# Other token blocks for the output projection and the FFN of a streaming encoder layer, and seven products for two more rows of the second FFN product

## The chip, the cores and the metric

The kernel runs on one core of a Trainium2 chip, in one launch. The metric is the device time of that execution in microseconds (us). Before the change its median is 2979.64 us over 3 runs (2978.55 to 2980.76).

## The reference

One inference step of one encoder layer, for a prompt of 2048 tokens and a sample of 64 tokens (one prompt, one sample, model width 1024), all in float32. The part that the change touches is the second half of the layer: the gated merge of the two branches, the output projection, and the SwiGLU FFN of inner width 2816 (22 rows of 128).

```
h = rms_norm(x, norm1_g) * (1 + sc1) + sh1
glu_a, glu_b, q, k, v, g_conv, g_attn = split(h @ w_in)
conv_out = conv_module(glu_a * sigmoid(glu_b))        # depthwise, 31 taps, LayerNorm, swish, @ w_conv_out
attn_out = band_attend(q, k, v) @ w_attn_out          # chunks of 64, own chunk and 8 before it

merged = sigmoid(g_conv) * conv_out + sigmoid(g_attn) * attn_out
x = x + gt1 * (merged @ w_o)                          # 1024 x 1024

h2 = rms_norm(x, norm2_g) * (1 + sc2) + sh2
gate, up = split(h2 @ w_ffn_in)                       # 1024 x 5632
x = x + gt2 * ((silu(gate) * up) @ w_ffn_out)         # 2816 x 1024
```

The prompt and the sample use the same weights, but each its own modulation (`sh`, `sc`, `gt`), and the sample has cached keys, values and convolution inputs. The outputs are the new x of both, and the states of convolution and attention.

## The kernel before

**Numbers.** Every float32 matrix is split into two fp32r parts, `hi` (ScalarE copies it) and `lo` (the difference, by VectorE or GpSimd). A product of two split matrices is three matmuls (`mm3`: hi·hi, hi·lo, lo·hi). The 64 sample tokens have a form of their own for the projections of token rows: hi and lo stand side by side as 128 columns, two matmuls (`mm2`) do all four products, and `fold` adds the two halves.

**Two parts.** The first part (up to about 1199 us) makes the modulation, the input projection, convolution, attention and gates, and leaves the branches' inputs and the gates in memory. The second part is a loop over `CBLOCKS`, three blocks of tokens in which the sample's tokens are 0 to 63 and the prompt's 64 to 2111:

```
CBLOCKS = [(0, 576), (576, 1344), (1344, 2112)]
```

The first block has 576 tokens, the sample and four tiles of 128; the other two have 768, six tiles. Each block goes through these stages.

- *Merge and output projection*, in two chunks of tiles. `load_mixed` and `gate_columns` load the inputs (`cin`, `tg`), `merge` multiplies them by the branch weights (`ca`) and joins the gates, and `wo` does the output projection into `pw`.
- *Columns.* For each tile a generator, `residual`, adds x, normalises the row, transposes it (TensorE), applies the modulation, and splits the result into operands for the FFN. The tokens of a block are cut in two halves (`half` columns: 288 in the first block, 384 in the others). From the two halves and the two halves of the model width come four quarters, and from them the seven operands `b11, b21, t2, t3, t1, t4, b22`.
- *Hand-over.* While the last columns are made, TensorE has ten products, `first` and `second`, of 12 matmuls each, for the first `EARLY` = 5 rows f (they need only `b11` and `b21`; their results are kept as `early`). Then the loop begins, which needs all seven operands.
- *Loop* over the 22 rows f, in pairs. `up` makes gate and up of row f by seven products instead of eight (Strassen's scheme in Winograd's form): 84 matmuls of `half` columns (`ps`), with sums of weights s1 to s4. VectorE and ScalarE combine the groups (`plus`, `silu`) and split the result, `hidden`, into `hid`. Between the products of a pair stand those of the pair before into the second FFN matrix (`pd`, 512 wide), whose results VectorE adds to `acc`. They are done in one of two ways. `down` and `add_down` do one product for each tile, column half and row. `down_pair`, where `seven(s, f)` says so, does a pair of rows and two halves of the tokens by seven products; `rest` makes the four sums S1 to S4 of the hidden columns (`sums`) for it, and GpSimd the sums t1 to t4 of the weights. Before, `seven` holds for f = 4 to 19 of the second and third block; its products are three tiles deep.
- *End of a block.* `add_down` or `add_last` adds the last rows, the modulation `gt2` and x, and sends the rows out; `scale` multiplies `acc` on GpSimd ahead of that.

**Weights.** `Weights` loads raw slabs (`wst`, `wup`, `wfo`), splits them (`whi`, `wlo`) and keeps up to five split slabs ahead of use. In the first block the sums s1 to s4 of the first FFN matrix are made on GpSimd (`ws`), used, and stored in memory (`sum_d`); the later blocks read them back. In the first block `W.hold` keeps the splits of these sums until the columns are done. The low half of a slab goes to GpSimd by default, and to VectorE in these cases, of which the last one matters here:

```
late = key[0] in ("up", "fo") and self.stream.load["pool"] - self.stream.load["pe"] > POOL_BEHIND   # 3000 ns
e, name = (self.dve, "dve") if on_dve or late else (self.gps, "pool")
```

**Order of the work.** Every engine runs its instructions in the order in which the program issues them. That order comes from a planner: `Stream` keeps a planned time for each engine (`load`), from a cost for each instruction; `after` and `when` shift it by dependences; generators wait in a `Lane` until TensorE's planned time has reached their due time. `weight_order` writes out the order of the slabs by hand. DMAs are issued on SP's queue.

**Buffers.** Eight banks of PSUM: four of tag `gp`, and `y0`, `z0`, `y1`, `z1`, in which the groups of `up` alternate. `down_pair` takes `zs` (one of `gp`, and `y1`, `z1`) and `ys` (of `gp`), one bank for each tile of a half, and uses each bank for several products in turn.

Of the kernel before, what the change touches and what calls it, by code (L numbers as in the profile page):

```python
# [35 lines left out]
CBLOCKS = [(0, 576), (576, 1344), (1344, 2112)]  # L36
# [41 lines left out]
def tile_chunks(lo, hi):  # L78

    tiles = token_tiles(lo, hi)  # L80
    t, n = tiles[(len(tiles) + 1) // 2 - 1]
    return [(lo, t + n), (t + n, hi)]
# [181 lines left out]
class Weights:  # L264
# [67 lines left out]
    @staticmethod  # L332
    def rows_of(op):

        return {"b11": (0,), "t1": (0,), "t3": (0, 1)}.get(op, (1,))
# [228 lines left out]
def seven(s, f):  # L564


    return s > 0 and 4 <= f < NF - 2
# [7 lines left out]
DOWN_OPERANDS = (("b11", "b21"), ("t3", "t2"), ("t1", "t4"), ("b22",))  # L575
# [8 lines left out]
def weight_order():  # L584
# [10 lines left out]
    for s in range(len(CBLOCKS)):  # L595
# [4 lines left out]
        for f in range(0, NF, 2):  # L600
            ops = up_operands(f) + up_operands(f + 1)
            for j in range(0, len(ops), 2):
                yield ("up", *ops[j : j + 2])
                if f >= 2 and seven(s, f - 2):
                    yield from (("dn", s, f - 2, *DOWN_OPERANDS[i]) for i in {0: (0,), 2: (1, 2), 4: (3,)}.get(j, ()))
                elif j == 0 and f >= 2 and f - 2 not in last_rows(s):
                    yield from (("fo", f - 2), ("fo", f - 1))
# [4 lines left out]
def streaming_layer(ctx: ExitStack, tc: tile.TileContext, I, O):  # L612
# [505 lines left out]
    def gate_columns(c0, c1, ct):  # L1118
        g = [half_piece(ct % 2, "tg") for _ in range(2)]
        for j in range(2):  # L1120
            nc.sync.dma_start(g[j][:, : c1 - c0], g_d[j, ct, :, c0:c1])
        return g

    def load_mixed(c0, c1, i):

        src = [[quarter("cin", i) for _ in range(2)] for _ in range(2)]
        for j, a in enumerate((c_d, o_d)):
            for l in range(2):
                nc.sync.dma_start(src[l][j][:, :, : c1 - c0].bitcast(F32), a[l, :, :, c0:c1].rearrange("c p t -> p c t"))
# [478 lines left out]
    for b, stage in ORDER:  # L1608
# [21 lines left out]
        elif stage == "g":  # L1630
            for g in gates(b, free):
# [6 lines left out]
                if g == SIDE_G and b == len(PBLOCKS) - 1:  # L1638
# [5 lines left out]
                    cs = tile_chunks(*CBLOCKS[0])[0]  # L1644
                    src = load_mixed(*cs, 0)
                    first_gates = gate_columns(*cs, 0)
# [43 lines left out]
    def merge(c0, c1, src, m, ahead, load):  # L1690
        n = c1 - c0
        cut = 0 if c0 else SMP
        for ct in range(KT):
# [15 lines left out]
            if ct + 2 < KT:  # L1709
                ahead.append(gate_columns(c0, c1, ct + 2))  # L1710
            dve.scalar_tensor_tensor(ps[1], ps[1], 2.0, t, ALU.mult, ALU.add)
            stream.after("act", "dve")
            hi = m[0][:, ct, cut : cut + n]
            act.activation(hi, ps[1], AF.Copy)
            stream.after("dve", "act")
            if cut:
                dve.tensor_tensor(m[0][:, ct, :cut], ps[1][:, :cut], hi[:, :cut].bitcast(F32), ALU.subtract)
            dve.tensor_tensor(m[1][:, ct, cut:n], ps[1][:, cut:], hi[:, cut:].bitcast(F32), ALU.subtract)
# [99 lines left out]

    c0, c1 = tile_chunks(*CBLOCKS[0])
    nxt = [first_gates, gate_columns(*c0, 1)]  # L1820
    srcs = [src]
    W.last_phase(wk, sum_d)
    for s, (lo, hi) in enumerate(CBLOCKS):
        tiles = token_tiles(lo, hi)
        half = (hi - lo) // 2
        gt1, groups, hs = {}, [], None
        chunks = tile_chunks(lo, hi)
        for i, (c0, c1) in enumerate(chunks):
            m = [wk.tile([P, KT, CW // 2], F32R, tag=f"m{j}", name="m") for j in range(2)]
            merge(c0, c1, srcs[i], m, nxt, (lambda: srcs.append(load_mixed(*chunks[1], 1))) if len(srcs) == 1 else None)  # L1830
            if c1 < hi:
                nxt = [gate_columns(c1, hi, ct) for ct in range(2)]
            else:
                turns.drain(groups[0], True)
            grp = [(t, n) for t, n in tiles if c0 <= t < c1]
            pss = [[row_bank(i, j) for j in range(2)] for i in range(len(grp))]
            if not groups:
                for which in {int(t < SMP) for t, _ in tiles}:
# [5 lines left out]
            def free():  # L1844
# [4 lines left out]
                residual(pss[i], t, n, gt1, t - lo, half, hs, free, c1 == hi, i) for i, (t, n) in enumerate(grp)  # L1849
# [7 lines left out]
            def wo(i, k):  # L1857
                (t, n), pp = grp[i], pss[i]
# [3 lines left out]
                c = slice(t - c0, t - c0 + n)  # L1862
                a = m[0][:, k, 0 if c0 else SMP :]
                for j in range(2):
                    f = slice(512 * j, 512 * j + 512)
                    if t < SMP:
                        mm2(pp[j], m[0][:, k, : 2 * SMP], wh[:, 0, f], wl[:, 0, f], k == 0, k == KT - 1)
                    else:
                        mm3(pp[j][:n], a[:, c], m[1][:, k, c], wh[:, 0, f], wl[:, 0, f], k == 0, k == KT - 1)
# [4 lines left out]
            shared = KT - 2 if not s and c1 == hi else 4  # L1874
# [3 lines left out]
            for i, (t, n) in enumerate(grp):  # L1878
                for k in range(shared, KT):
                    wo(i, k)  # L1880
                while gens[i] in xs:
                    turns.push()
                next(gens[i])
                turns.add(gens[i])
# [39 lines left out]

        def hidden(f, i, ps):
            h = hid_of(f)
            c = slice(i * half, (i + 1) * half)
            stream.after("act", "dve")
            if s:
                split(h[:, 0, c], h[:, 1, c], ps)  # L1930
                return
            hi = h[:, 0, SMP:][:, c]
            act.activation(hi, ps, AF.Copy)
            stream.after("dve", "act")
            cut = 0 if i else SMP
            if cut:
                dve.tensor_tensor(h[:, 0, :cut], ps[:, :cut], hi[:, :cut].bitcast(F32), ALU.subtract)
            dve.tensor_tensor(h[:, 1, c][:, cut:], ps[:, cut:], hi[:, cut:].bitcast(F32), ALU.subtract)
# [80 lines left out]
        def rest(f, z, y):  # L2019
# [5 lines left out]
            if "t" not in sums:  # L2025
                sums["t"] = wk.tile([P, 4, 2, CW // 2], F32R, tag="m1", name="sums")
            at = lambda i: [sums["t"][:, i, l, :half] for l in range(2)]
            if f % 2 == 0:
                sums["a21"], sums["s3"] = (
                    wk.tile([P, CW // 2], F32, tag=name, name=name, bufs=1)[:, :half] for name in ("a21", "s3")  # L2030
# [266 lines left out]
```

## Time and profile before

| | |
|---|---|
| median of 3 runs | 2979.64 us (2978.55 to 2980.76) |
| the profiled execution's own time | 2979.5 us |
| its span, first to last instruction | 2977.7 us |
| mean granted clock of TensorE | 0.995 |
| second part | from about 1199 us to the end |
| first block: merge and projection, hand-over, loop | 1199 to 1301, 1301 to 1390, 1390 to about 1717 us |
| hand-over of the second and of the third block | around 1865 and 2495 us |

The profile's first part gives the busy time of each engine over the span. PE is TensorE's matmuls, PEld its weight loads, which run beside the matmuls; DVE is VectorE, ACT ScalarE, POOL GpSimd, SP the engine that issues DMAs. The chain that ended last goes back from the last instruction to what released each step. A window row gives the busy time and count of every engine in a stretch, then TensorE's granted clock (1 is full speed), the DMA engines' busy share and GB/s. A row of waits reads: waiting engine and tile, released by which engine and tile, us in total, how many times, longest. A row of the timeline reads: start, duration, engine, operation, with the idle time ahead of it and its releaser in brackets. Rows by form give count, busy us, mean ns of one, and the idle time ahead of them. All operations are recorded by one helper, so all lines are L102; the tiles' names tell them apart.

### The profile page before, as it was taken

What the parts mean: (1) busy time and instruction counts of PE and PEld (TensorE: products, weight loads), DVE (VectorE), ACT (ScalarE), POOL (GpSimd) and SP (SyncE); (2) the same over time, 40 slices, a digit from 0 to 9 for tenths busy, and PEclk for the clock granted to TensorE, in tenths of its full rate; (3) what the DMA queues carried; (4) which work ended last, traced back from release to release, by engine and by line L of the source; (5) the groups of instructions that cost most, each with busy time, mean ns of one, the idle gap of its engine ahead of it and who ended that gap; (6) DMA issues with size and microseconds to landing.
All of it is one profiled execution on the core that took longest, in us unless ns stands there. A gap on an engine that the chain in (4) does not pass through costs nothing.

```text
span 2977.7 us, 44838 instructions
## 1 busy us (share of the span) xinstructions
PE 2900.2 (97%) x16199; PEld 2593.1 (87%) x16199; DVE 2025.9 (68%) x3637; ACT 1356.8 (46%) x2441; POOL 1127.7 (38%) x727
## 2 busy tenths in 40 slices
PE   7999899999999999989999999999999999999999
PEld 4899777787888888888999999999999999999998
DVE  5797677767856886577777755666666557466666
ACT  2345642662456257464444345534444345344442
POOL 0201310111011102454466443255666741465667
PEclk9999999999999999999999999999999999999999
DMA  8889889878987798885444786333333975333333
GB/s 290 300 286 310 270 279 312 284 251 274 306 283 224 267 263 278 262 288 175 145 145 159 244 263 235 116 95 106 114 113 113 316 239 184 93 95 114 114 103 128
DMA packets 467723, 628.05 MB, mean 211 GB/s; under 512 B 36276, under 2 KB 314664, under 8 KB 467501
## 3 DMA queue, kind: packets, MB, share of 16 engines
q1 hardware_dynamic: 453456, 605.58, 62.8%
q10 hardware_dynamic: 14045, 19.60, 1.9%
q8 instruction: 127, 2.08, 0.3%
q14 instruction: 95, 0.78, 0.1%
HBM read 476.53 MB, written 148.54 MB: 210 GB/s over the span
## 4 chain that ended last, share of the span: by engine, by line
PE 82%; DVE 7%; DMA 4%; ACT 2%; issue 2%; POOL 2%; SPq 0%; ACTq 0%; POOLq 0%; DVEq 0%
PE ps L102 53%; PE pd L102 16%; PE pw L102 6%; DVE y L102 2%; PE sc L102 2%; PE po L102 2%; PE ptp L102 2%; DVE wlo L102 1%; PE pt L102 1%; DMA kk<-k_d 1%; ACT whi L102 1%; PE pa L102 1%; POOL r L102 1%; DVE pw L102 1%; DMA wst<-in_w_in 0%
## 5 line engine op out<-in xcount | busy, mean ns | idle before, releaser
L102 PE MATMUL ps<-t,whi 128*128 128x384 f32 (+1 forms) x2112 | 503.1, 322 | 8.7 <-ACT t L102 4.9
L102 POOL TENSOR_TENSOR wlo<-wst,whi 128x1024 fp32r<-128x1024 f32 (+1 forms) x156 | 356.4, 2294 | 279.0 <-ACT whi L102 262.6
L102 ACT ACTIVATE whi<-wst 128x1024 fp32r<-128x1024 f32 (+1 forms) x263 | 256.8, 979 | 331.2 <-PE ps L102 119.8
L102 PE MATMUL ps<-b,whi 128*128 128x384 f32 (+1 forms) x1584 | 381.7, 326 | 7.0 <-DVE early L102 3.6
L102 PEld LDWEIGHTS ps<-t,whi 128*128 128x128 f32 x2112 | 367.8, 188 | 16.3 <-ACT t L102 5.1
L102 DVE SCALAR_TENSOR_TENSOR y<-u,wd,y 128x512 f32<-128x512 f32 (+1 forms) x480 | 369.0, 773 | 6.3
L102 PE MATMUL ps<-hh,whi 128*128 128x512 f32 (+2 forms) x992 | 361.7, 365 | 0.0
L102 DVE TENSOR_TENSOR acc<-acc,pd 128x512 f32<-128x512 f32 x464 | 311.7, 685 | 62.7 <-PE pd L102 60.2
L102 PE MATMUL ps<-hl,whi 128*128 128x512 f32 (+2 forms) x992 | 345.6, 348 | 0.0
L102 PE MATMUL ps<-hh,wlo 128*128 128x512 f32 (+2 forms) x992 | 345.4, 348 | 0.0
L102 PE MATMUL ps<-t,wlo 128*128 128x384 f32 (+1 forms) x1056 | 339.4, 322 | 0.8 <-POOL wlo L102 0.7
L102 PE MATMUL pd<-whi,hid 128*128 128x512 f32 x972 | 314.8, 390 | 0.0
L102 PEld LDWEIGHTS ps<-b,whi 128*128 128x128 f32 x1584 | 278.7, 189 | 13.1 <-DVE early L102 4.5
L102 POOL TENSOR_TENSOR r<-t,mhalf 128x1 f32<-128x1 f32 (+3 forms) x68 | 83.6, 1232 | 462.1 <-DVE t L102 457.0
L102 PE MATMUL ps<-b,wlo 128*128 128x384 f32 (+1 forms) x792 | 257.3, 325 | 0.0
L102 ACT ACTIVATE pr<-pr,sm 128x640 f32<-128x640 f32 (+3 forms) x272 | 200.1, 747 | 112.1 <-DVE sm L102 109.5
L102 PEld LDWEIGHTS pd<-whi,hid 128*128 128x128 f32 x972 | 182.5, 188 | 37.7 <-ACT hid L102 0.7
L102 PEld LDWEIGHTS ps<-hh,wlo 128*128 128x128 f32 x992 | 186.7, 188 | 21.6
L102 PEld LDWEIGHTS ps<-hh,whi 128*128 128x128 f32 x992 | 187.2, 189 | 18.5 <-issue 1.6
L102 PEld LDWEIGHTS ps<-hl,whi 128*128 128x128 f32 x992 | 187.5, 189 | 15.5 <-issue 1.4
L102 PEld LDWEIGHTS ps<-t,wlo 128*128 128x128 f32 x1056 | 198.2, 188 | 2.2 <-POOL wlo L102 1.3
L102 PE MATMUL pd<-wlo,hid 128*128 128x512 f32 x508 | 198.6, 391 | 0.0
(226 smaller groups left out, 6170.6 us busy)
## 6 DMA issues: line engine op xcount, KB each, us to landing
whi<-w_din_h SPq DMA_DIRECT2D x72, 512.0 KB, 6.5
wlo<-w_din_l SPq DMA_DIRECT2D x72, 512.0 KB, 8.4
wst<-sum_d SPq DMA_DIRECT2D x132, 256.0 KB, 2.7
wfo<-in_w_ffn_out SPq DMA_DIRECT2D x64, 512.0 KB, 3.2
wmod<-in_w_ada SPq DMA_DIRECT2D x46, 512.0 KB, 6.5
sum_d<-ws SPq DMA_DIRECT2D x88, 256.0 KB, 2.8
wst<-in_w_ffn_in SPq DMA_DIRECT2D x84, 256.0 KB, 3.1
wst<-in_w_in SPq DMA_DIRECT2D x40, 512.0 KB, 8.8
```

The source lines that it names most:

```text
L102: self.last = f(*args, **kw)
```

## The change

The second part's blocks become 768, 768 and 576 tokens, and the sample moves from the first block to the last, where it stands third among five tiles, across the middle. `seven` starts at f = 2 and holds in the last two blocks, also in the last one with the sample. There the halves have 288 columns, of which `side` = 32 belong to the sample; the seven products run over the `wide` = 256 inner columns of the prompt (two tiles deep), and the sample's rows get `mm2` products of their own (`sample`), for which the slab with `b22` gets an eighth operand, `b12`. `hidden_sample` splits the sample's 32 columns of each half. In `rest`, the split of S3 moves from the even row to the odd one. `scale`, `add_last` and `add_down` follow: the rows `gt` for the sample are loaded in the last block, and `add_last` does its last rows with `mm2` and a fold.

```diff
-CBLOCKS = [(0, 576), (576, 1344), (1344, 2112)]
+CBLOCKS = [(64, 832), (832, 1600), (1600, 2112)]
+MIXED = 2
...
+def block_tiles(s):
+    tiles = [(t, P, t - CBLOCKS[s][0]) for t in range(*CBLOCKS[s], P)]
+    if s == MIXED:
+        tiles = tiles[:2] + [(0, SMP, 2 * P)] + [(t, n, a + SMP) for t, n, a in tiles[2:]]
+    return tiles
+
+def block_chunks(s):
+    lo, hi = CBLOCKS[s]
+    n = (hi - lo) // 2
+    return [[(0, lo, n)] + [(n, 0, SMP)] * (s == MIXED), [(0, lo + n, n)]]
...
 def seven(s, f):
-    return s > 0 and 4 <= f < NF - 2
+    return s > 0 and 2 <= f < NF - 2
...
+def down_operands(s):
+    return ("b11", "b21"), ("t3", "t2"), ("t1", "t4"), ("b22", "b12") if s == MIXED else ("b22",)
...
-            shared = KT - 2 if not s and c1 == hi else 4
+            shared = KT - 2 if len(grp) < 3 else 4
...
+        side = half - 2 * P if s == MIXED else 0
+        wide = half - side
+        inner = [slice(0, wide), slice(side, half)]
...
         def hidden(f, i, ps):
...
+            split(h[:, 0, rows_at[i]], h[:, 1, rows_at[i]], ps[:, inner[i]])
+            hidden_sample(f, i, ps)
...
         def rest(f, z, y):
...
             if f % 2 == 0:
+                hidden_sample(f, 1, whole)
...
-                split(*at(2), y)
                 act.activation(sums["s3"], y, AF.Copy)
                 return
-            hidden(f, 1, y)
-            t = bank("gp")
+            hidden(f, 1, whole)
+            split(*at(2), sums["s3"])
+            t = bank("gp")[:, :wide]
...
         def down_pair(f):
...
-            n = len(tiles) // 2
+            n = wide // P
...
+            def sample(ps, w, es, j):
+                for e, (h, l) in zip(es, ((t[0][:, i], t[1][:, i]) for t, i in w)):
+                    mm2(ps, hid[0][:, e, 0, both], h, l, e == es[0], e == es[1])
+                stream.after("dve", "pe")
+                dst = acc[n][:, 512 * j : 512 * j + 512]
+                dve.tensor_tensor(dst, dst, ps, ALU.add)
...
             products(ys, a11, w, 0, True, False, 0, 0)
             yield
-            zs += [bank_of(tag, "pd") for tag in ("y1", "z1")]
+            zs += [bank_of(tag, "pd") for tag in ("y1", "z1")[: n - 1]]
             products(zs, a12, w, 1, True, True, 0, 0)
+            if s == MIXED:
+                sample(bank_of("gp", "pd"), ((w, 0), (w, 1)), (0, 1), 0)
...
             products(zs, s3, w, 0, True, False, 1, 1)
             yield
             products(ys, s2, w, 1, False, False, 1, 0)
             W.done()
             w = W.get(("dn", s, f, *ops[2]))
             products(ys, s1, w, 0, False, False, 1, 1)
             products(zs, a22, w, 1, False, True, 1, 0)
             W.done()
             yield
             w = W.get(("dn", s, f, *ops[3]))
             products(ys, s4, w, 0, False, True, 0, 1)
+            if s == MIXED:
+                sample(bank_of("z1", "pd"), ((w, 0), (w, 1)), (1, 0), 1)
```

More of the change, by code (lines that the diff above doesn't have):

```diff
@@ L1688, in token_row, with merge @@
         return wk.tile([P, D], F32, tag="row", name=name, bufs=6)
-    def merge(c0, c1, src, m, ahead, load):
-        n = c1 - c0
-        cut = 0 if c0 else SMP
+    def merge(chunk, src, m, ahead, load):
+        n = width(chunk)
+        cut = n - (SMP if len(chunk) > 1 else 0)
         for ct in range(KT):
```

180 lines of the change are left out of this document (96 added, 84 removed).

## The prediction

> **What bounds the kernel now.** I read the page first (span, engines, chain), then the windows stage by stage, then TensorE's waits in the stretches that the change touches, and last the durations by form.
>
> ```profile
> PE 2900.2 (97%) x16199; PEld 2593.1 (87%) x16199; DVE 2025.9 (68%) x3637; ACT 1356.8 (46%) x2441; POOL 1127.7 (38%) x727
> ...
> PE 82%; DVE 7%; DMA 4%; ACT 2%; issue 2%; POOL 2%; SPq 0%; ACTq 0%; POOLq 0%; DVEq 0%
> ```
>
> TensorE is busy for 97% of the span and holds 82% of the chain that ended last. So only two things can move the time: the number and pitch of matmuls, and the few places where TensorE stands. The windows show where in the second part it stands: the hand-over of its first block (1301 to 1390), that block's loop (1390 to 1690), and, for comparison, the loop of the last block (2520 to 2940).
>
> ```profile
> core 0: us, PE busy (x) PEld busy (x) DVE busy (x) ACT busy (x) POOL busy (x), PEclk, DMA share, GB/s
> 1301.00:1390.00 89.00, 77.61 (x488) 71.70 (x487) 68.76 (x122) 49.67 (x96) 40.37 (x31) 0.96 0.74 255
> 1390.00:1690.00 300.00, 297.47 (x1911) 276.74 (x1910) 217.20 (x343) 124.82 (x255) 172.97 (x113) 1.00 0.48 154
> 2520.00:2940.00 420.00, 419.64 (x2201) 392.71 (x2201) 261.26 (x428) 183.06 (x310) 252.41 (x152) 1.00 0.33 104
> 1318.70:1322.30 3.60, 3.35 (x13) 2.92 (x13) 3.10 (x7) 2.23 (x8) 0.00 (x0) 0.53 1.03 396
> 1329.00:1332.40 3.40, 3.34 (x14) 3.35 (x15) 3.40 (x6) 1.12 (x3) 2.70 (x3) 0.52 0.50 185
> ```
>
> The hand-over leaves TensorE idle for 89.00 − 77.61 = 11.4 us, the first loop for 2.5 us, the last block's loop for 0.4 us. The last two rows are stretches right behind idle time, with a granted clock of 0.53 and 0.52: 3.60 × 0.47 + 3.40 × 0.48 = 3.3 us more. The hand-over thus loses 11.4 + 3.3 = 14.7 us. TensorE's waits there, and then at the hand-over to the third block (2470 to 2520):
>
> ```profile
> PE ps L102 <- ACT t L102: 4.9, 1, 4.9
> PE ps L102 <- DVE early L102: 2.6, 1, 2.6
> PE ps L102 <- DVE u L102: 1.6, 1, 1.6
> PE ps L102 <- DVE v L102: 1.4, 1, 1.4
> PE ps L102 <- ACT early L102: 0.8, 2, 0.5
> ```
>
> ```profile
> PE ps L102 <- DVE early L102: 0.5, 1, 0.5
> PE ps L102 <- POOL wlo L102: 0.3, 1, 0.3
> PE ps L102 <- ACT early L102: 0.2, 1, 0.2
> ```
>
> 11.3 us of named waits in the first block stand against 1.0 us in the third. The first makes its weight sums on GpSimd and is 576 tokens wide; the third reads the sums back and is 768 wide. Half of the difference in width is what the change takes away.
>
> **The terms, against the profiled execution (2979.5 us, 1.8 us more than the page's span of 2977.7; the median of the runs, 2979.64, is 0.14 above).**
>
> *Matmuls.* In the order of instructions the first FFN product, merge and output projection keep their matmuls at the same widths, only in another order of blocks. The second FFN product goes from 616, 720 and 720 matmuls to 792, 711 and 562: 2056 to 2065, +9. The wider first block has six full tiles by eight products; the two more rows by seven products and the narrower last block nearly pay for it. The pitch, from 32 and then 20 matmuls in a row, and from 8 at the third width:
>
> ```profile
> 1499.79 0.39 PE L102 MATMUL pd<-whi,hid 128*128 128x512 f32 x1
> ...
> 1507.05 0.39 PE L102 MATMUL pd<-whi,hid 128*128 128x512 f32 x1
> 1507.27 0.42 PE L102 MATMUL ps<-t,whi 128*128 128x288 f32 x2
> ...
> 1509.90 0.29 PE L102 MATMUL ps<-t,wlo 128*128 128x288 f32 x1
> ```
>
> ```profile
> 2199.96 0.51 PE L102 MATMUL ps<-t,whi 128*128 128x384 f32 x2
> ...
> 2201.35 0.33 PE L102 MATMUL ps<-t,wlo 128*128 128x384 f32 x1
> ```
>
> 7.26 / 32 = 0.227 us, 2.63 / 20 = 0.1315 us, 1.39 / 8 = 0.174 us. So 9 × 0.227 = **+2.0 us**: the arithmetic alone makes the kernel slightly slower, and every gain must come from waits.
>
> *Hand-over of the first block.* While ScalarE and VectorE turn the last tiles into columns and their sums, TensorE has the ten products of `first` and `second` to do, 12 matmuls each. At 384 columns these 120 matmuls last 120 × (0.174 − 0.1315) = 5.1 us longer. The second of the long waits, and what ScalarE waits for ahead of it:
>
> ```profile
> 1316.24 1.15 ACT L102 ACTIVATE whi<-ws 128x512 fp32r<-128x512 f32 x2 [2.32 <-POOL ws L102]
> 1318.72 0.73 PE L102 MATMUL ps<-b,whi 128*128 128x288 f32 x2 [2.63 <-DVE early L102]
> ```
>
> The waits are steps of one chain (columns, then operands `t`, then the first groups of the loop), so 5.1 us more cover takes 5.1 of 11.3 us off; both half-clock stretches follow waits of 2.6 us and more, and I let their 3.3 us go with them: −8.4, taken as **−8.5 us**. One end is −13.7 (the first block becomes like the third, 14.7 − 1.0). The other is 0: the second group now has three tiles instead of two, and in the new order ScalarE has three `whi<-ws`, which wait for GpSimd's sums as above, ahead of the columns of the last two tiles. What is late next in either case is that column work. [...]
>
> *Loop of the first block.* Its 2.5 us of idle are VectorE and ScalarE behind a 288-wide step; at 384 every product lasts a third longer, the loops of that width idle 0.4 us in 420. **−2.5 us**, from 0 to −6 (stalls that the modelled ends cover).
>
> *Hand-over of the last block*, now the 288-wide one: the third block's 1.0 us of waits with 5.1 us less cover, but without sums to make. **+1.5 us**, from −1 (sums already stored, five tiles instead of six) to +7 (all of the 5.1 us as a wait, and 1.7 us of half clock behind it). Its sample rows come as extra DMAs of a few per block on SP; they are issued among the loads of the merge, ahead of need by a chunk, and cost nothing unless they delay `cin`, which is in the +7.
>
> *Loop of the last block.* This is the dear unknown. `split` gives the low half of an `up` or `fo` slab to VectorE where GpSimd's planned load is over 3 us ahead of TensorE. With a 288-wide loop that is nearly always: the order of instructions has 80 `wlo` on VectorE in the last block (79 of 1024 elements) where the block before had 25, and the first block 129, mostly of 512. The durations:
>
> ```profile
> L102 DVE TENSOR_TENSOR wlo<-ws,whi 128x512 fp32r<-128x512 f32 x47 | 44.6, 953 | 3.8 <-ACT whi L102 2.6
> ...
> L102 DVE TENSOR_TENSOR hid<-ps,hid 128x288 fp32r<-128x288 f32 x18 | 8.2, 456 | 7.2 <-ACT hid L102 7.2
> ...
> L102 DVE TENSOR_TENSOR hid<-ps,hid 128x224 fp32r<-128x224 f32 x17 | 6.4, 378 | 0.0
> ```
>
> ```profile
> L102 DVE TENSOR_TENSOR acc<-acc,pd 128x512 f32<-128x512 f32 x178 | 120.3, 686 | 18.1 <-PE pd L102 17.0
> ...
> L102 DVE TENSOR_TENSOR wlo<-wst,whi 128x1024 fp32r<-128x1024 f32 x8 | 11.2, 1395 | 2.9 <-ACT whi L102 2.8
> ```
>
> ```profile
> 2702.37 1.28 DVE L102 TENSOR_TENSOR acc<-acc,pd 128x512 f32<-128x512 f32 x2
> ```
>
> A pair of rows f costs TensorE 168 matmuls of the first product and 50 of the second: 168 × 0.1315 + 50 × 0.227 = 33.4 us. VectorE does in it 16 `acc` × 0.686 = 11.0, 7 `wlo` × 1.395 = 9.8, 14 operations of 288 × 0.456 = 6.4, 11 of 256 (between 0.378 and 0.456, so 0.42) = 4.6, and 4 of 32 columns (taken at 0.2, about half of the 0.378) = 0.8: 32.6 us, 98%. Operations queued behind one another overlap, though: two `acc` take 1.28 us where 2 × 0.686 = 1.37, 0.09 less each. With most of 52 so queued that gives back up to 4.6 us: 28 to 30 us, 85 to 90%, where the last block now has 261.26 / 420 = 62% and the first 217.20 / 300 = 72%. So I expect VectorE to keep up, but late adds to bite in one place: with two tiles, the product by S1 re-uses the banks of the product by S2 after only one group of three matmuls (3 × 0.227 = 0.68 us), while the add that must come between lasts 0.69. A `wlo` ahead of it in VectorE's queue makes TensorE wait 0.3 to 1.0 us, and behind that wait the whole loop is queued. At the low end, 9 pairs × 0.33 = **+3.0 us**; from 0 (the add starts in time) to +18 (rival A). The split of S3 that moves to the odd row is used a whole row later, 84 × 0.1315 = 11 us: nothing. GpSimd's own work falls with the slabs it loses.
>
> [...]
>
> *Tail.*
>
> ```profile
> 2971.96 0.39 PE L102 MATMUL pd<-whi,hid 128*128 128x512 f32 x1
> ...
> 2973.63 0.69 DVE L102 TENSOR_TENSOR acc<-acc,pd 128x512 f32<-128x512 f32 x1
> ```
>
> VectorE now ends 2.0 us behind TensorE's last matmul. The tail's matmuls fall from 72 to 56 (16.3 to 12.7 us), its VectorE operations from 24 to 22 (by 0.6 to 0.69 us each, 13.3 to 15 us), so VectorE falls behind: **+1.0 us**, 0 to +2.5.
>
> **Sum:** 2.0 − 8.5 − 2.5 + 1.5 + 3.0 + 1.0 = −3.5 us: **2976.0 us**.
>
> **Rivals.**
>
> *A, VectorE becomes the bound of the last block (slower).* For it: 98% by durations, and the trace has VectorE idle before work it must wait for (18.1 / 178 = 0.10 us before each `acc`, 7.2 / 18 = 0.40 before each 288-wide `hid`): 32.6 + 16 × 0.10 + 4 × 0.40 = 35.8 us a pair, 2.4 more than TensorE; with a little of the overlap given back, about 2. Nine pairs: +18 in place of +3: **2991 us**. Against it: those idle times shrink as soon as a queue stands. It decides when VectorE's busy share in the pairs exceeds some 95%.
>
> *B, the hand-over vanishes and VectorE keeps up.* 2.0 − 13.7 − 2.5, the other terms at nothing: −14.2, **2965 us**. For it: the third block's 1.0 us of waits at the same width. Against it: the third reads stored sums, the first still makes them.
>
> *C, the loss only moves with the 288 columns to the last block.* −8.5 becomes −7 and +1.5 becomes +7, the rest as forecast: 2.0 − 7 − 2.5 + 7 + 3 + 1 = +3.5, **2983 us**. Against it: the second and third blocks make no sums.
>
> That the change does not do what it says is no rival: the counts in the order of instructions are those of its words.
>
> **How the numbers follow.** 0.2% is 6.0 us, about what a measurement of this kernel tells from no change. The forecast's own case (2969 to 2982) gets 0.42, of which 0.13 lies below 2973.6; B 0.27, A 0.24, C 0.07. Faster: 0.27 + 0.13 = 0.40; same: 0.29 + 0.07 = 0.36; slower: 0.24. Range: 2963 (the middle of B and a little beyond) to 2993 (past the middle of A), which leaves out the far halves of A and B, some 0.2.
>
> **What would show it.** In the profile after: TensorE's waits in the first hand-over at 3 to 7 us and no clock of 0.5 in it; 0.5 us or less idle in that block's loop; about 1.5 to 3 us of waits ahead of the last block's loop; in that loop, waits of `pd` matmuls for VectorE's `acc`, a few tenths each, once a pair, and VectorE busy at 85 to 92%. It is wrong if the first hand-over still waits over 10 us, if `ps` matmuls of the last loop wait for VectorE's plus operations or its `wlo` in every row (A), or if a wait on a DMA appears in the last merge.

## The result, and the profile after

The change makes the kernel slower: 3001.61 us median (2999.62 to 3005.45, 4 runs) against 2979.10 us (2978.04 to 2980.76, 4 runs) before, a ratio of 1.0077 with a 95% interval of 1.0059 to 1.0094. The prediction was 2976.0 us, 2963 to 2993.

The page of the kernel after, engines and chain:

```profile
PE 2906.9 (97%) x16208; PEld 2592.6 (86%) x16208; DVE 2058.2 (69%) x3667; ACT 1372.3 (46%) x2516; POOL 1127.4 (38%) x747
...
PE 77%; DVE 11%; DMA 4%; ACT 3%; issue 3%; POOL 1%; SPq 1%; ACTq 0%; DVEq 0%; POOLq 0%
```

TensorE's busy time grew by 6.7 us, and its share of the chain fell from 82% to 77%, that of VectorE rose from 7% to 11%. The windows by stage: the first hand-over with the start of its loop, that loop, the last block's merge, its hand-over with the start of the loop, its pairs of seven products, and two stretches right behind idle time.

```profile
core 0: us, PE busy (x) PEld busy (x) DVE busy (x) ACT busy (x) POOL busy (x), PEclk, DMA share, GB/s
1331.60:1400.00 68.40, 57.99 (x308) 53.95 (x308) 58.59 (x92) 37.95 (x75) 35.21 (x26) 0.98 0.69 234
1400.00:1818.00 418.00, 417.40 (x2203) 392.54 (x2202) 212.45 (x317) 151.54 (x280) 244.99 (x169) 1.00 0.38 123
2478.00:2590.00 112.00, 107.58 (x634) 96.94 (x633) 64.47 (x131) 51.75 (x83) 56.95 (x28) 0.98 0.90 289
2590.00:2652.00 62.00, 52.34 (x339) 48.90 (x338) 40.58 (x74) 36.13 (x67) 14.25 (x9) 0.94 0.49 167
2690.00:2960.00 270.00, 265.85 (x1678) 242.09 (x1677) 242.00 (x401) 147.40 (x304) 149.98 (x97) 1.00 0.43 134
1362.90:1366.40 3.50, 3.48 (x11) 3.48 (x12) 3.50 (x7) 1.58 (x3) 0.00 (x0) 0.54 0.00 0
2612.40:2615.60 3.20, 3.20 (x13) 3.20 (x14) 3.20 (x6) 0.60 (x1) 0.00 (x0) 0.50 0.00 0
```

TensorE stands idle for 10.4 us in the first hand-over, almost the 11.4 of before, and now for 9.7 us in the last block's, where it waited about 1 us before. The last block's pairs lose 4.2 us of 270, and VectorE is busy there for 242 of 270 us, 90%. TensorE's waits in the first hand-over, and then from 2560 to 2690 us:

```profile
PE ps L115 <- ACT early L115: 2.5, 2, 1.4
PE ps L115 <- ACT t L115: 2.2, 1, 2.2
PE ps L115 <- DVE t L115: 1.9, 1, 1.9
PE ps L115 <- DVE u L115: 1.7, 2, 1.4
PE ps L115 <- DVE early L115: 1.6, 2, 1.3
...
```

```profile
PE ps L115 <- ACT t L115: 8.3, 1, 8.3
PE ps L115 <- DMA wlo<-w_dfi_l: 1.1, 1, 1.1
...
```

**Where the time went.** The first part of the kernel, untouched, took from 1190 to 1199 us in the profiled executions of this study. So I also compare the second part alone, from the first merge matmul (`ps<-cin`) to TensorE's last one: 1772.7 us before (1199.2 to 2972.0), 1796.5 us after (1195.2 to 2991.8), +23.8. By blocks, from one block's first merge matmul to the next one's (for the last block, to the end of TensorE's last matmul): 515.8, 628.5 and 628.9 us before, 656.2, 627.2 and 513.6 us after. With the pitch of 0.227 us for the matmuls of the second product (616, 720, 720 before, 792, 711, 562 after), a wide first block should have taken 628.9 + 72 × 0.227 = 645.2 us and took 11.0 more; a narrow last one 515.8 − 54 × 0.227 = 503.5 us and took 10.1 more; the middle one is 0.7 over its 626.5. With the 9 matmuls (2.0) that is 23.8.

A finer table takes the time from each matmul's start to the next one's, less the pitch of its width (0.2268, 0.1735, 0.1305 us for 512, 384, 288), summed by stage; I call it the loss (matmuls missing from a trace count in it, and 0.001 us on the pitch of 288 is 1.8 us in a loop). "Hand-over" is `first` and `second` with the transposes between them, and the first 40 us of the loop:

| us lost | merge, projection | hand-over | rest of loop | end |
|---|---|---|---|---|
| before, first block (576) | 3.5 | 11.1 + 4.4 | 10.0 | 0.0 |
| before, second block (768) | 1.0 | 1.7 + 0.6 | 4.1 | 0.4 |
| before, third block (768) | 1.3 | 1.7 + 0.7 | 4.1 | 0.4 |
| after, first block (768) | 1.3 | 6.5 + 8.4 | 2.9 | 0.0 |
| after, second block (768) | 1.1 | 1.7 + 0.7 | 4.8 | 0.4 |
| after, last block (576) | 7.7 | 10.8 + 2.1 | 17.5 | 0.9 |

All hand-overs together lose 10.0 us more than before (30.2 and 20.2), the loops 7.0 (25.2 and 18.2), the merges 4.3 (10.1 and 5.8), the ends 0.5; with the matmuls' 2.0 that is the 23.8. Each trace is one execution, so differences of a few us in a stage of the last block tell little: e6 and e11 below, whose edits leave that block alone, run it in 509.5 and 508.3 us instead of 513.6; there its hand-over loses 12.5 and 13.0 us (12.9 in the changed kernel), its loop 16.4 and 13.7, its merge 5.1 and 6.1.

The wide block did not lose less by going first than the narrow one had, and the narrow one lost nearly as much again going last.

### The profile page after: what moved, and what is told of

Read it like the earlier page. It is cut to its first block, busy times and chain, and to the rows that moved or that the text cites. A ratio compares the mean times of both kernels' runs of the same rounds, so it can differ in the third digit from the quotient of the medians.

```text
span 2997.5 us, 44910 instructions
## 1 busy us (share of the span) xinstructions
PE 2906.9 (97%) x16208; PEld 2592.6 (86%) x16208; DVE 2058.2 (69%) x3667; ACT 1372.3 (46%) x2516; POOL 1127.4 (38%) x747
## 4 chain that ended last, share of the span: by engine, by line
PE 77%; DVE 11%; DMA 4%; ACT 3%; issue 3%; POOL 1%; SPq 1%; ACTq 0%; DVEq 0%; POOLq 0%
PE ps L115 50%; PE pd L115 13%; PE pw L115 6%; DVE wlo L115 3%; DVE y L115 2%; PE sc L115 2%; PE po L115 2%; PE ptp L115 2%; DVE acc L115 1%; PE pt L115 1%; DVE ps L115 1%; PE pa L115 1%; ACT whi L115 1%; POOL r L115 1%; DVE pw L115 1%
## 5 line engine op out<-in xcount | busy, mean ns | idle before, releaser
L115 PE MATMUL ps<-t,whi 128*128 128x384 f32 (+1 forms) x2112 | 505.3, 323 | 19.4 <-ACT t L115 10.5
L115 ACT ACTIVATE whi<-wst 128x1024 fp32r<-128x1024 f32 (+1 forms) x272 | 264.7, 979 | 285.8 <-PE ps L115 115.7
L115 PEld LDWEIGHTS ps<-t,whi 128*128 128x128 f32 x2112 | 369.1, 188 | 28.4 <-ACT t L115 11.1
L115 POOL TENSOR_TENSOR wlo<-wst,whi 128x1024 fp32r<-128x1024 f32 (+1 forms) x130 | 276.8, 2139 | 217.1 <-ACT whi L115 180.7
L115 DVE TENSOR_TENSOR acc<-acc,pd 128x512 f32<-128x512 f32 x451 | 298.6, 683 | 65.7 <-PE pd L115 64.5
L115 PE MATMUL pd<-whi,hid 128*128 128x512 f32 x1002 | 322.9, 390 | 0.3 <-DVE acc L115 0.3
L115 PEld LDWEIGHTS ps<-b,whi 128*128 128x128 f32 x1584 | 278.3, 189 | 12.6 <-ACT early L115 3.9
L115 DVE TENSOR_TENSOR wlo<-wst,whi 128x1024 fp32r<-128x1024 f32 (+1 forms) x142 | 201.6, 1421 | 91.5 <-ACT whi L115 90.1
L115 POOL TENSOR_TENSOR wlo<-ws,whi 128x512 fp32r<-128x512 f32 x113 | 145.7, 1307 | 209.3 <-ACT whi L115 208.0
L115 POOL TENSOR_TENSOR wlo<-wfo,whi 128x512 fp32r<-128x512 f32 (+1 forms) x92 | 161.9, 1774 | 135.6 <-ACT whi L115 135.6
```

What stands on the lines that cost most here:

```text
L115: self.last = f(*args, **kw)
```

## The experiments

Each median is that of the experiment's own runs, and each ratio is to the kernel before, run again beside them; "second part" is the length defined above, of the profiled execution (1796.5 us after).

**Two parts of the change.** e1 is the kernel before with the rows alone, e2 the changed kernel with the blocks alone.

```diff
# e1, on the kernel before (S3's split on the odd row for f = 2 only)
-    return s > 0 and 4 <= f < NF - 2
+    return s > 0 and 2 <= f < NF - 2
# e2, on the changed kernel (S3's split on the even row)
-    return s > 0 and 2 <= f < NF - 2
+    return s > 0 and 4 <= f < NF - 2
```

> The kernel before with one part of the change alone: seven products from row 2 in the two blocks that have them, blocks as before. 18 matmuls of 512 fewer (2056 to 2038). Theory 1 (the loss comes from VectorE's queue in a 288-wide last block) and theory 2 (the loss is the 288-wide block's hand-over) both say: 18 x 0.227 = 4.1 us faster than before, about 2975. Rival (the second product's new pair and the S3 split taken from SBUF cost as much as they save): 2979 or more.

Measured: 2974.98 us, ratio 0.9984 (0.9974 to 0.9994), second part 1771.3 us. The rows are a small gain; the median agrees with 18 × 0.227, the second part shows 1.4 of the 4.1 us.

> The changed kernel with seven products from row 4 only and S3 split on the even row from PSUM, as before: the blocks' part of the change alone. 15 matmuls more than the changed kernel (+3.4 us). If the blocks carry the loss (theories 1 and 2): 2999 to 3005, at least 20 us over before. If the pair of rows 2 and 3 carries it: near 2980.

Measured: 3002.91 us, ratio 1.0081 (1.0066 to 1.0096), second part 1800.0 us, 3.5 over the changed kernel for 15 matmuls more. The blocks carry the whole loss.

**VectorE as the bound.** e3 takes 0.75 us a pair off VectorE; e4 moves low halves from VectorE to GpSimd, 33 of the last block's 79 by the trace.

```diff
# e3
             if f % 2 == 0:
...
+                if "t" in sums:
+                    split(*at(2), y)
                 act.activation(sums["s3"], y, AF.Copy)
...
-            split(*at(2), sums["s3"])
+            if f == first_seven + 1:
+                split(*at(2), sums["s3"])
# e4, in split
+            late = late and not (i > self.last_start and i % 2)
```

> The changed kernel with S3 split on the even row straight from PSUM in all pairs but the first of a block. In the changed kernel's last block that split's second half, from two SBUF operands, took 1.17 us on VectorE where the other three of 256 columns took 0.42. Theory 1 (VectorE's queue bounds the last loop): 8 x 0.75 = 6 us of VectorE less, so 2996 to 2999. Theory 2: no change, 3001.

Measured: 3004.01 us, ratio 1.0085 (1.0070 to 1.0100), second part 1799.7 us. No gain, although VectorE's busy time in the last block's pairs fell from 242.0 to 231.9 us.

> The changed kernel, but in the last block every second slab of the first product that would go to VectorE stays on GpSimd (34 low halves of 1024 moved back, 1.65 us each on VectorE, 2.4 on GpSimd). Theory 1: VectorE falls from 89% to about 75% of that loop, its excess of some 13 us mostly goes: 2988 to 2993. Theory 2: the loop's loss is not VectorE's, 3000 or more. Rival within theory 1 (GpSimd becomes the bound): waits of matmuls for wlo of GpSimd, 3001 or more.

Measured: 3002.21 us, ratio 1.0077 (1.0062 to 1.0092), second part 1796.8 us. No gain, although the load moved as meant. The last block's pairs in e4, and TensorE's waits in them:

```profile
2690.00:2960.00 270.00, 263.42 (x1686) 241.97 (x1684) 211.48 (x377) 148.78 (x307) 194.39 (x122) 1.00 0.43 133
```

```profile
PE pd L115 <- DVE acc L115: 2.4, 6, 0.4
PE ps L115 <- DVE acc L115: 2.3, 3, 0.8
PE ps L115 <- ACT u L115: 1.8, 2, 1.5
```

VectorE fell from 90% to 78%, and TensorE still waits for its `acc`. A load that can be lowered by an eighth without effect was not the bound: theory 1 falls.

**Banks used again after one group.** In the trace after, the place looks like this (TensorE, then VectorE at the same time):

```profile
2851.93 0.39 PE L115 MATMUL pd<-wlo,hid 128*128 128x512 f32 x1
2852.49 0.50 PE L115 MATMUL pd<-whi,sums 128*128 128x512 f32 x1 [0.17 <-DVE acc L115]
```

```profile
2848.92 0.69 DVE L115 TENSOR_TENSOR acc<-acc,pd 128x512 f32<-128x512 f32 x1
2849.53 1.94 DVE L115 TENSOR_TENSOR wlo<-wst,whi 128x1024 fp32r<-128x1024 f32 x1
2851.40 0.45 DVE L115 TENSOR_TENSOR ps<-ps,u 128x288 f32<-128x288 f32 x1
2851.76 1.27 DVE L115 TENSOR_TENSOR acc<-acc,pd 128x512 f32<-128x512 f32 x2
```

The second matmul, the first with S1, is the one that waits. Two matmuls of the next product (`hid`) already stand ahead of it, so five matmuls, 1.1 us, lie between the two uses of the bank, not the three that the prediction counted; it is so in all six pairs where TensorE waits for `acc`. A `wlo` of 1.94 us stands ahead of the add for which TensorE waits. e7 does not shorten it; it only lets TensorE do another product first.

```diff
+            products(zs, a22, w, 1, False, True, 1, 0)
             products(ys, s1, w, 0, False, False, 1, 1)
-            products(zs, a22, w, 1, False, True, 1, 0)
```

> The changed kernel, with the product of a22 by t4 ahead of that of S1 by t1 in each pair, so that no bank is used again after one group only. The trace after shows 0.33 + 0.11 us once a pair at that place. If it is the bank: 9 x 0.44 = 4 us faster, 2997.6. If VectorE is late in any case (theory 1), the wait moves to the next group: 3001.

Measured: 2995.77 us, ratio 1.0055 (1.0038 to 1.0073), 5.8 below the changed kernel; second part 1789.4 us, 7.1 less; the loss in the rest of the loop falls from 17.5 to 8.0 us. The pairs in e7, and all that TensorE waits for in them:

```profile
2690.00:2960.00 270.00, 269.09 (x1736) 251.08 (x1735) 242.54 (x412) 150.86 (x309) 155.62 (x102) 1.00 0.45 140
```

```profile
PE ps L115 <- ACT u L115: 0.7, 3, 0.3
```

VectorE is as busy as in the changed kernel (242.54 and 242.00 us of 270), and TensorE hardly waits. So 9.5 us of the loop's loss hung on the distance between two uses of a bank. In the table's terms 5.3 us of the changed kernel's loss stood ahead of matmuls with S1 to S4 (0.4 in e7), and 2.5 us where `ps` goes over from `b` to `t` (0.1 in e7). The 8.0 us that stay are less than the 288-wide loop lost before (10.0).

**The last hand-over.** e5 queues the first products that need `t` behind the last `second`; in the changed kernel a matmul that reads `t` stood ahead of 48 that read none.

```diff
+            with tc.issue_after(pe.last.ins) if not f else nullcontext():
                 if not f:
                     z = bank("z0")
                     step(z, "s3", "t3", True, False)
                 step(y, "s2", "t2", f < EARLY, False)
```

> The changed kernel, with the first two products of row 0 queued on TensorE behind the last `second` product. In the changed kernel's last block one matmul that needs the operand t stands ahead of 48 ready matmuls of `first` and `second` and waits 8.3 us. Theory 3 (the loss at the last hand-over is the order of TensorE's queue): the 48 matmuls x 0.1315 = 6.3 us go into that wait and the half clock behind it goes too: 2993 to 2995. Rival (the columns are late and the order is indifferent): 3001.

Measured: 3002.34 us, ratio 1.0073 (1.0058 to 1.0088), second part 1799.5 us. No gain, and the trace tells why: now the sixth product, which needs no `t`, waits as long.

```profile
2601.89 0.29 PE L115 MATMUL ps<-b,wlo 128*128 128x288 f32 x1
2610.49 0.82 PE L115 MATMUL ps<-b,whi 128*128 128x288 f32 x2 [8.31 <-ACT t L115]
```

It is `first` of row 3, into bank `z1`. That bank is also one of the two in which the second group's first tile is projected, transposed and split; ScalarE's last `t` from it sets it free. e9 gives rows 3 and 4 free banks, on top of e5; e10, on the changed kernel, lets that tile end earlier.

```diff
# e9, on e5
-            x = bank(("y0", "z0", "y0", "z1", "y1")[f])
+            x = bank("gp" if f > 2 and len(groups[1]) < 3 else ("y0", "z0", "y0", "z1", "y1")[f])
# e10
-            shared = KT - 2 if len(grp) < 3 else 4
+            shared = KT - 2 if len(grp) < 3 and not s else 4
```

> e5_products_first, and where the second group of a block has two tiles, `first` of rows 3 and 4 takes banks of tag gp instead of z1 and y1. In e5 the sixth product waited 8.31 us, although it needs no t: its bank z1 still holds the columns of the group's first tile. Theory 5 (that bank is what the last hand-over waits for): the five products left, 60 x 0.1315 = 7.9 us, go into the wait, 1 to 3 us of it remain: 2994 to 2996. Rival (the operands t themselves are as late): the wait stays whole ahead of the first product with t, 3001.

Measured: 2998.18 us (2987.63 to 2999.32, 5 runs), ratio 1.0051 (1.0033 to 1.0069); second part 1790.2 us, 6.3 less, of which the hand-over has 3.3 (its loss is 9.6 us); the runs spread over 11.7 us, so the median adds nothing to that. The wait of 8.3 us is gone, but less is won than was expected, since others follow it; TensorE's waits from 2585 to 2660 us are these:

```profile
PE ps L115 <- DVE t L115: 2.2, 2, 1.3
PE ps L115 <- ACT t L115: 2.1, 1, 2.1
PE ps L115 <- DMA wlo<-w_dfi_l: 1.2, 1, 1.2
```

> The changed kernel, with 4 instead of 6 of 8 steps of the output projection shared between the two tiles of the last block's second group. The group's first tile then ends 24 instead of 12 matmuls (5.4 instead of 2.7 us) ahead of the group's end, where in a group of three it ends 48 matmuls (10.9 us) ahead. Theory 5's other half (the tile that holds the bank is late because its group is short): the wait of 8.3 falls by 2.7 and the half clock behind it stays: 2998 to 2999. Rival: 3001.

Measured: 2994.88 us, ratio 1.0051 (1.0035 to 1.0068), 6.7 below the changed kernel, more than expected; second part 1793.5 us, 3.0 less. No wait for `t` of ScalarE is left in the hand-over: its loss falls from 12.9 to 10.2 us, by the 2.7 us that were expected (the rest of the median's gain isn't found in the profiled execution). What TensorE waits for in its place, from 2590 to 2660 us:

```profile
PE ps L115 <- DMA whi<-w_dfi_h: 2.9, 1, 2.9
PE ps L115 <- DVE pw L115: 1.3, 1, 1.3
...
```

The bank and the late tile are both at work: e9 and e10 each take about 3 us off the hand-over's loss, both together (e13, below) 7.7 of 12.9.

**The first hand-over.** There ScalarE's queue holds splits of weight sums between the column work; its waits from 1330 to 1378 us:

```profile
ACT whi L115 <- POOL ws L115: 10.1, 4, 3.2
ACT t L115 <- DVE pw L115: 4.2, 3, 2.1
ACT xn L115 <- POOL r L115: 2.2, 1, 2.2
```

e6 queues those splits behind the columns (and holds them back while the last columns are issued); e11 makes no sums at all, neither when they are needed nor ahead of it.

```diff
# e6
...
+            W.columns = lambda ins=act.last.ins: tc.issue_after(ins)      # after the last column
...
+            with self.columns() if i in self.first else nullcontext():
                 self.act.activation(hi[:, c], src, AF.Copy)
...
# e11, in operand
-            with self.behind():
-                self.gps.tensor_tensor(t, x, y, e)
+            t = (u, g, g, g)[j][:, 4:] if j == 3 else (u, g, g, g)[j][:, :4]
...
-        if not self.hold and i in self.first and all(...):
+        if False and all(...):
```

> The changed kernel, with ScalarE's splits of the first block's weight sums queued behind its last instruction for the columns. In the changed kernel's first hand-over ScalarE waits 10.1 us for GpSimd's sums, with column work queued behind. Theory 4 (the first hand-over is bound by ScalarE standing in those waits, not by cover): 6 to 10 us faster, 2992 to 2996. Rival (the splits, now late, are what the loop waits for): 3001 or more.

Measured: 3007.02 us, ratio 1.0091 (1.0076 to 1.0107), slower by 5; the first block takes 661.9 us instead of 656.2. TensorE's waits there:

```profile
PE ps L115 <- ACT whi L115: 6.8, 1, 6.8
PE ps L115 <- DVE u L115: 5.1, 1, 5.1
...
```

The last `t` came 31.4 us behind the start of the hand-over instead of 38.6, and the splits became what the loop waits for: the rival was right.

> The changed kernel without the 88 sums of the first FFN matrix on GpSimd: a raw quarter is taken and stored in the place of each, so the result is another. Everything else is as it was. Theory 6 (what the first block's hand-over waits for is the making of sums, whatever its width): the first block's loss falls from 18 us to the 7 us of the second, 2990 to 2992. Rival (the first block loses because it is the first: inputs, raw loads, columns): no change, 3001.

Measured: 2992.04 us, ratio 1.0037 (1.0025 to 1.0049), 9.6 below the changed kernel; second part 1782.6 us, 13.9 less. The first block is 8.6 us shorter: its loss from the hand-over to the loop's end falls from 17.8 to 9.5 us, and its waits to these:

```profile
PE ps L115 <- ACT early L115: 1.2, 1, 1.2
PE ps L115 <- DVE t L115: 1.0, 1, 1.0
PE ps L115 <- DVE early L115: 0.9, 2, 0.6
PE ps L115 <- ACT t L115: 0.5, 1, 0.5
```

So the sums are about half of what the first block loses from the hand-over on. The other 5.3 us of the second part stand in the last block, which makes no sums; their cause stays open. The edit also changes the planner's choice: 32 low halves of 512 go from VectorE to GpSimd in the first block, though only one of them in the 70 us from the start of the hand-over.

**Do the causes add up, and why did they cost less before?** e13 joins e7, e9 and e10; e15 is e13 without the sums; e14 is the changed code with `CBLOCKS = [(64, 576), (576, 1344), (1344, 2112)]` and `MIXED = 0`.

> The changed kernel with e7 (a22 by t4 ahead of S1 by t1), e9 (products first, free banks) and e10 (4 shared steps) together. If the losses are separate: the second part (first merge matmul to TensorE's last), 1797.0 us in the changed kernel, falls by 7 for the loop and by 6 to 9 for the hand-over to 1781 to 1784; median 2985 to 2989. If VectorE is the bound of that block after all, less than 8 us in all: 2994 or more.

Measured: 2986.38 us, ratio 1.0028 (1.0018 to 1.0037), second part 1780.9 us, as forecast for separate losses. The last hand-over loses 3.9 + 1.3 us, the rest of the loop 9.9. The pairs from 2690 to 2950 us:

```profile
2690.00:2950.00 260.00, 258.45 (x1652) 239.91 (x1651) 233.69 (x395) 143.79 (x293) 149.87 (x97) 1.00 0.44 138
```

VectorE is still at 90%.

> e13 without the 88 sums on GpSimd, as in e11 (raw quarters in their place, another result). If the three causes add up: e13 less the 8 to 10 us of e11, second part 1770 to 1775, median 2975 to 2980, at the level of the kernel before. If one of them was covering another: 2983 or more.

Measured: 2978.82 us, ratio 1.0003 (0.9993 to 1.0013), second part 1775.4 us. The median is in the range that was forecast for causes that add up, and at the level of the kernel before; the second part is just past its range, 5.5 us below e13. By blocks, the first is 8.0 us shorter than in e13, almost the 8.6 of e11, and the last one 2.6 us longer, within what it varies by. (The kernel before does make its sums; of the 2.7 us left against it in the second part 2.0 are the nine matmuls.)

> The changed code, with the mixed block of 576 tokens first and eight products in it, seven from row 2 in the other two: 18 matmuls fewer than before. If the loss is the order of the blocks (sums and two-tile group in two blocks instead of one): as e1, 2973 to 2977. If the changed code around the sample costs by itself: 2980 or more.

Measured: 2982.59 us, ratio 1.0007 (0.9997 to 1.0017), second part 1777.8 us. That is the second answer, past 2980: the changed code costs something by itself. The second part runs from 1771.3 (e1) over 1777.8 (e14) to 1796.5 us (changed kernel). The last step, 18.7 us, is the order of the blocks: 27 matmuls (6.1) and 12.6 us of waits. The first step, 6.5 us, is the changed code with the blocks as before, and it stands in one place, the first block's merge, whose loss is 9.6 us where e1 has 3.4. TensorE's waits there in e14, and below them those of the kernel before:

```profile
PE ps L115 <- DVE t L115: 3.3, 3, 1.9
PE ps L115 <- DVE o_p L115: 1.4, 1, 1.4
PE pw L115 <- POOL wlo L115: 1.3, 2, 1.0
...
```

```profile
PE ps L102 <- DVE o_p L102: 1.4, 1, 1.4
PE ps L102 <- DVE m L102: 0.4, 1, 0.4
```

That is the changed kernel's last merge too (7.7 us lost): with the sample as the third tile of the first group, the second merge waits for VectorE's `t`, and a little for a load:

```profile
PE ps L115 <- DVE t L115: 3.6, 2, 2.5
PE ps L115 <- DMA cin<-o_d: 0.8, 1, 0.8
...
```

What in the sample's work VectorE does ahead of it I did not test.

**The kernel before, mended.** e8 is e1 with e5 and e6, e12 is e1 with e5 and e9, e16 is e1 with 4 shared steps in its first block, which has a group of two tiles as well.

> The kernel before with seven products from row 2 (as e1_seven_alone, 2975), and both orders of e5 and e6 in its first block of 576 tokens: the first products of row 0 behind the last `second`, the splits of sums behind the columns. That hand-over waits 11.3 us and loses 3.3 to half clock. Theories 3 and 4: 6 to 10 us below e1, 2965 to 2969. Rival (the column chain itself is too long for 120 matmuls of 288): 2973 to 2975.

Measured: 2978.70 us, ratio 0.9998 (0.9988 to 1.0007), second part 1772.5 us. Neither theory's gain came.

> e1_seven_alone (2975) with the same two edits as e9 in its first block of 576 tokens, whose second group has two tiles too. If the bank of the first tile is the wait there as well (4.9 us on ACT t): 2969 to 2972. If the sums are what is late in the first block (theory 6), the wait only moves: 2974 to 2976.

Measured: 2976.37 us, ratio 0.9992 (0.9982 to 1.0002), second part 1769.4 us, 1.9 below e1. The first hand-over loses 3.2 + 11.6 us, where e1 loses 11.2 + 5.3. TensorE's waits from 1290 to 1390 us:

```profile
PE ps L102 <- DVE u L102: 3.3, 1, 3.3
PE ps L102 <- DVE t L102: 2.0, 1, 2.0
...
```

> e1_seven_alone with 4 instead of 6 shared steps in the first block's second group, which has two tiles. If its bank is late there too: 2 to 4 us below e1, 2971 to 2973. If the sums are what that block waits for: 2975, as e1.

Measured: 2978.20 us, ratio 1.0000 (0.9991 to 1.0010), second part 1771.7 us.

None has a lower median than e1. In e12 the bank's wait went, and most of its 8 us came back at once as waits behind it: in that block the bank and something else are late over the same stretch, and it pays once. That the other is the sums fits ScalarE's 9.0 us of waits for them in e12 (6.0 in e1), but the kernel before wasn't run without its sums. This is where the expected gain went. The kernel before had both waits in one block; the change put the sums into the first block and the group of two tiles into the last, and pays for each. By the medians the fastest version found is e1, 4 us below the kernel before, and its interval is the only one that lies below 1. How much of that the rows give stays open: e16 has a second part only 0.4 us longer and a median 3.2 us higher.

## Why the prediction was wrong

The second part was to fall by 3.5 us and grew by 23.8. The 27.3 us between are 7.9 in the first hand-over, 9.0 in the last one, 10.4 in the last loop and 4.3 in the merges, less 4.6 in the first loop; the small terms make the rest (0.3).

**What held.** The count of matmuls and its 2.0 us. The sign of the first loop's term: its 10.0 us of loss became 2.9, 7.1 less, where 2.5 less were forecast and 6 at most. The place of the last loop's loss, the S1 product behind S2, and that a `wlo` ahead of the add is what makes it bite. VectorE's share of 85 to 92% (measured 90%).

**Hand-over of the first block, forecast −8.5 us.** Loss before 15.5 us, after 14.9: a gain of 0.6 us. This step failed. It took the waits for one chain that more cover shortens. But ScalarE stood 10.1 us in waits for sums (6.6 us before, from 1300 to 1350 us), with a third tile's columns to do besides; both ends of that term were at or below zero, and the prediction named the three `whi<-ws` only as a bound. e11 shows the sums' part, 8.3 us from the hand-over to the loop's end. Two of the prediction's own signs of being wrong came: 10.9 us of waits in this hand-over, and a wait for a load (`cin`) in the last merge.

**Hand-over of the last block, forecast +1.5 us, at most +7.** Loss 12.9 us, against 2.4 in the wide third block: +10.5 us. The step reasoned that without sums there is nothing to wait for. It left out which bank each product takes and how far ahead of the group's end its first tile is done: 2.7 us in a group of two with 6 shared steps, 10.9 us in a group of three with 4, 8.2 us less of a lead. e13, which mends both, takes 7.7 of the 12.9 us off. The row for it was in the trace of before, where the 288-wide block waits 4.9 us on ACT `t`; I read it as a late operand, and e12 shows that the bank was late there as well.

**Loop of the last block, forecast +3.0 us.** Loss 17.5 us, against 4.1 in the third block: +13.4. The mechanism was right and the size was off, twice. The 288-wide loop has a loss of its own wherever it stands (10.0 us in the first block before); I took it off the first block and did not add it to the last. And the bank's wait is not 9 × 0.33: e7, which removes it, takes 9.5 us from the loop's loss and 7.1 from the second part: the waits ahead of the S products came to 5.3 us in the table's terms, not 3.0, and most of the waits of `ps` matmuls went with them.

**Rival A** gave the right side and half of the size (2991, 12 us over before, where 22.5 came), for a wrong reason: VectorE was never the bound, as e4 (78% busy, no gain) and e7 (90% busy, no waits) show. **Rival C**, that the loss only moves, was nearest to what happened, at a chance of 0.07: the loss did not move, it split, and each half kept nearly the whole price.

**The merge** of the last block had no term of its own: it lost 7.7 us where the third block lost 1.3, and the first block's merge gave back 2.2 of that. **The tail** is within its bounds: VectorE ends 2.3 us behind TensorE's last matmul, 2.0 before.

**The clock, and GpSimd beside VectorE.** The prediction had no clock of 0.5 left in the first hand-over. The trace after has 0.54 over 3.5 us there, behind two waits of 2.2 and 1.9 us with one matmul between, and 0.50 over 3.2 us in the last hand-over, behind the wait of 8.3 us. S3's split lasted longer with GpSimd beside it (1.38 to 1.48 us, against 0.41 and 0.43; last section), but that did not decide the time: e3 took 10 us off VectorE without a gain.

## What to carry to other kernels

Waits that lie over each other in one stage are paid once; an edit that spreads their causes over two stages pays for each, and mending one of them in place gains little (1.9 us of second part in e12). For every product that is to cover a chain, look up which bank it writes and who holds that bank until when: a wait named after a data tile can be a wait for its bank (8.31 us in e5). When a tile count shrinks, check how many groups lie between two uses of the same bank, and reorder products before blaming the engine that empties it.

## What the runs showed of the hardware

In the last block's pairs of the changed kernel (2690 to 2960 us) two of VectorE's operations, both with two SBUF inputs, lasted longer when a GpSimd instruction ran beside them: S3's split and the low halves. S3's split took 0.41 and 0.43 us the two times with GpSimd idle, 1.38 to 1.48 us the six times when it began 0.1 to 0.2 us behind a GpSimd `wlo`. Two of the eight, and GpSimd beside the second:

```profile
2695.05 0.41 DVE L115 TENSOR_TENSOR sums<-s,sums 128x256 fp32r<-128x256 f32 x1
...
2765.86 1.40 DVE L115 TENSOR_TENSOR sums<-s,sums 128x256 fp32r<-128x256 f32 x1
```

```profile
2765.69 2.73 POOL L115 TENSOR_TENSOR wlo<-ws,whi 128x512 fp32r<-128x512 f32 x2 [1.68 <-ACT whi L115]
```

So the 0.75 us (1.167 on average over the eight, against 0.420 for the three splits from PSUM) came where GpSimd ran beside the split, and not with the reading from SBUF alone: in e7, where the split falls elsewhere, the same eight took 0.458 us on average. The rows of the changed kernel and of e7:

```profile
L115 DVE TENSOR_TENSOR sums<-s,sums 128x256 fp32r<-128x256 f32 x8 | 9.3, 1167 | 0.9 <-ACT sums L115 0.9
```

```profile
L115 DVE TENSOR_TENSOR sums<-s,sums 128x256 fp32r<-128x256 f32 x8 | 3.7, 458 | 0.5 <-ACT sums L115 0.5
```

In the same pairs `acc`, with one input in PSUM, took 0.67 to 0.69 us with GpSimd beside it or not. The low halves of 1024 took 1.21 to 1.23 us alone and 1.83 on average when GpSimd ran for 0.5 us or more of them. Their mean was 1.65 us over 46, and 1.95 us over 24 in e4, where GpSimd is busy for 194 instead of 150 us. So moving 22 of them away gave back 29 us and not 36. In the prediction I had taken 1.395 us, a mean over eight in the kernel before, of which one had GpSimd beside it and took 2.58 us and the other seven took 1.23.
